# Eight of 128 first keys of an expert lookup: from gathered rows to dense products

## The chip, the cores and the metric

The kernel runs on one core of a Trainium2 chip. Times are device microseconds (us) of one execution. The core's engines are TensorE (PE, with its weight loads shown as PEld), VectorE (DVE), ScalarE (ACT), GpSimd (Pool) and SyncE (SP); 16 DMA engines move data between the chip's memory and the core.

## What is computed

The kernel computes two transformer layers and then a third block, for 256 tokens of width 1024. All but the last part of the last block is untouched here. That last part is a layer of product keys: each token has 8 heads, each head picks 16 of 16,384 experts, an expert's number being 128 times its first key plus its second key. For each of the 128 picks of a token, the kernel takes the dot product of the token with the expert's row of `expert_u`, applies Gelu, multiplies by the gate, and adds the expert's row of `expert_v` with that weight.

```
    e1 = jnp.take_along_axis(i1, ic // PEER_TOPK, axis=-1)
    e2 = jnp.take_along_axis(i2, ic % PEER_TOPK, axis=-1)
    idx = (e1 * N_KEYS + e2).reshape(T, PEER_HEADS * PEER_TOPK)
    gate = jax.nn.softmax(vc, axis=-1).reshape(T, PEER_HEADS * PEER_TOPK)

    def block(args):
        xb, ib, gb = args
        u = expert_u[ib]
        pre = jnp.einsum('td,tkd->tk', xb, u).astype(jnp.float32)
        a = jax.nn.gelu(pre, approximate=False) * gb
        return jnp.einsum('tk,tkd->td', a, expert_v[ib])
```

Each of `expert_u` and `expert_v` is 128 x 128 x 1024 numbers of 4 bytes, 64 MB.

## The kernel before

**First product.** `expert_u` is read whole. For each first key e, `u_step(e)` (L1764 and on) multiplies the 128 rows of that key with all 256 tokens on PE, in two float parts of each row (`whi` from ACT at L70, `wlo` from DVE at L73), and writes the result into the tile `GS`: GS[second key, first key, token]. PE sets the pace there.

**Second product.** `expert_v` is not read whole. There are 64 steps s of four tokens each (token s and the ones 32, 64 and 96 further on for s below 32, the second 128 tokens after that). A step has these parts:

- `gather(s)` (L1804): Pool issues four indirect DMAs, one for each token, each fetching 128 rows of 4 KB, one for each partition. They land in slots; 14 slots are taken in turn (the buffers `raw`, `whi` and `wlo` of the first product, shown as vt, and a tile vx of four).
- `spread(s)` (L1815): four small bfloat16 products copy each token's second keys to all partitions, and DVE compares them with the partition number (L86), which gives a one-hot tile of 128 x 512 under the tag `o2`.
- `extract(s)` (L1826): four products in float32 pick the picked second keys out of `GS`; then DVE picks the first key by four multiplications with a sum (L90), multiplies (L73), ACT applies Gelu (L67), DVE multiplies by the gate and makes the weight tile `w32` (L73).
- `apply(s)` (L1843): eight float32 products of 128 x 32 weights with 128 x 512 gathered values, in PSUM accumulators `acc[j][half]`, for token half j.

`store(j)` (L1848 to L1852) loads the residual `xr` on SP's queue, adds the accumulator on DVE and stores the sum. `store(0)` stands at step 31 and `store(1)` after the last step. `xr` takes buffers of the tag `o2`, of which there are three.

The order of PE, DVE, ACT and Pool is that in which the code is written: each of these engines works through its list in order. In a step the code says spread(s+2), extract(s+1), apply(s), gather(s+3). A Pool gather waits for its slot, and gather i also for the landing of gather i - 8.

## Time and profile before

| | us |
|---|---|
| median of three timed runs | 1536.12 (1535.79 to 1536.47) |
| the profiled execution: its time | 1537.89 |
| its span, first to last instruction | 1536.2 |
| first gather starts | 1182.02 |
| last gather starts | 1520.04 |

Share of the span in which each engine is busy: PE 96%, PE's weight loads 73%, DVE 69%, ACT 43%, Pool 26%. The first product takes the time up to about 1196 us, the second product the remaining 340 us, with its first gathers issued a little ahead. The shares are means over stages with different limits, so a stage is read by stretches, by timelines and by what each engine waits for. Busy time of PE is modelled: pipelined products that wait inside a run count as busy.

### The profile page before, as it was taken

What the parts mean: (1) busy time and instruction counts of PE and PEld (TensorE: products, weight loads), DVE (VectorE), ACT (ScalarE), POOL (GpSimd) and SP (SyncE); (2) the same over time, 40 slices, a digit from 0 to 9 for tenths busy, and PEclk for the clock granted to TensorE, in tenths of its full rate; (3) what the DMA queues carried; (4) which work ended last, traced back from release to release, by engine and by line L of the source; (5) the groups of instructions that cost most, each with busy time, mean ns of one, the idle gap of its engine ahead of it and who ended that gap; (6) DMA issues with size and microseconds to landing.
All of it is one profiled execution on the core that took longest, in us unless ns stands there. A gap on an engine that the chain in (4) does not pass through costs nothing.

```text
span 1536.2 us, 23739 instructions
## 1 busy us (share of the span) xinstructions
PE 1474.2 (96%) x8634; PEld 1126.9 (73%) x8634; DVE 1059.9 (69%) x2519; ACT 668.0 (43%) x1248; POOL 391.7 (26%) x516
## 2 busy tenths in 40 slices
PE   6689999999999999999999999999999999999998
PEld 5568788878988888887888888888888544444443
DVE  7887877675566676776569888999555555555554
ACT  5356555565775555647755445444444000000000
POOL 1820100010100000031110002404000777677764
PEclk9889999999999999999999999999999999999999
DMA  8514655554345555453354555555555999999998
GB/s 319 153 37 164 218 190 191 184 176 138 111 137 185 187 191 189 165 187 123 115 187 161 191 184 179 192 181 191 190 182 184 354 409 408 403 408 409 408 391 333
DMA packets 97389, 341.98 MB, mean 223 GB/s; under 512 B 12016, under 2 KB 15220, under 8 KB 96376
## 3 DMA queue, kind: packets, MB, share of 16 engines
q1 hardware_dynamic: 60120, 206.18, 39.2%
q0 software_dynamic: 36864, 134.23, 22.2%
q8 instruction: 68, 1.11, 0.3%
q14 instruction: 49, 0.40, 0.1%
q10 hardware_dynamic: 288, 0.05, 0.0%
HBM read 337.80 MB, written 2.62 MB: 222 GB/s over the span
## 4 chain that ended last, share of the span: by engine, by line
PE 69%; DMA 16%; DVE 6%; issue 4%; POOL 3%; ACT 2%; SPq 0%; POOLq 0%; DVEq 0%; ACTq 0%
PE mm L375 27%; PE mm L376 14%; DMA vt<-in_ev_dram,pidx 12%; PE acc L385 4%; PE acc L386 4%; PE acc L384 4%; PE mm L367 3%; DMA vx<-in_ev_dram,pidx 3%; PE acc L1843 2%; PE acc L247 1%; DVE wlo L73 1%; POOL vt L1804 1%; PE mm L384 1%; PE mm L385 1%; PE mm L386 1%
## 5 line engine op out<-in xcount | busy, mean ns | idle before, releaser
L375 PE MATMUL mm<-x,whi 128*128 128x512 f32 x1808 | 641.8, 399 | 0.0
L73 DVE TENSOR_TENSOR wlo<-raw,whi 128x1024 fp32r<-128x1024 f32 x345 | 434.2, 1260 | 207.6 <-ACT whi L70 194.9
L376 PE MATMUL mm<-x,wlo 128*128 128x256 f32 x1808 | 507.4, 281 | 2.0 <-DVE wlo L73 2.0
L70 ACT ACTIVATE whi<-raw 128x1024 fp32r<-128x1024 f32 x347 | 366.2, 1057 | 186.6 <-issue 92.0
L375 PEld LDWEIGHTS mm<-x,whi 128*128 128x128 f32 x1808 | 340.4, 188 | 82.5
L376 PEld LDWEIGHTS mm<-x,wlo 128*128 128x128 f32 x1808 | 341.8, 189 | 4.5 <-DVE wlo L73 2.8
L1804 POOL DMA_INDIRECT vt<-in_ev_dram,pidx x184 | 172.5, 938 | 187.1 <-DVE wlo L73 117.0
L1843 PE MATMUL acc<-vt,w 128*32 128x512 f32 x736 | 157.9, 603 | 9.0 <-DMA vt<-in_ev_dram,pidx 4.7
L67 ACT ACTIVATE pk<-pk 128x4 f32<-128x4 f32 x64 | 13.2, 205 | 314.2 <-DVE pk L73 314.2
L70 ACT ACTIVATE gs<-mm 128x256 f32<-128x256 f32 x142 | 54.6, 384 | 207.5 <-PE mm L376 207.5
L90 DVE SCALAR_TENSOR_TENSOR jk<-c,pe,mm 128x128 f32<-128x128 f32 x256 | 89.0, 348 | 72.3 <-PE mm L1826 65.4
L1826 PE MATMUL mm<-gs,o 128*128 128x128 f32 x512 | 124.6, 398 | 1.2 <-DVE o L86 1.2
L73 POOL TENSOR_TENSOR nv<-nss 128x2 f32<-128x2 f32 x5 | 1.0, 195 | 434.3 <-ACT nsq L67 434.3
L1826 PEld LDWEIGHTS mm<-gs,o 128*128 128x128 f32 x512 | 98.2, 202 | 6.2 <-issue 2.2
L1843 PEld LDWEIGHTS acc<-vt,w 128*32 128x32 f32 x736 | 27.7, 108 | 97.4 <-DMA vt<-in_ev_dram,pidx 52.6
L86 DVE TENSOR_SCALAR o<-mm,pcol 128x512 f32<-128x512 f32 x64 | 47.9, 750 | 52.0 <-PE mm L1815 52.0
L1843 PE MATMUL acc<-vx,w 128*32 128x512 f32 x288 | 71.6, 603 | 2.9 <-DMA vx<-in_ev_dram,pidx 1.3
L1804 POOL DMA_INDIRECT vx<-in_ev_dram,pidx x72 | 67.6, 938 | 23.4 <-issue 15.5
L385 PE MATMUL acc<-whi,fhl 128*128 128x512 f32 x176 | 69.9, 397 | 1.4 <-DVE fhl L73 1.4
L384 PE MATMUL acc<-whi,fhh 128*128 128x512 f32 x176 | 69.7, 400 | 1.1 <-ACT fhh L70 1.1
L386 PE MATMUL acc<-wlo,fhh 128*128 128x512 f32 x176 | 69.7, 396 | 0.0
L73 DVE TENSOR_TENSOR gs<-gs,mm 128x256 f32<-128x256 f32 x142 | 58.7, 413 | 10.8 <-ACT gs L70 10.7
(520 smaller groups left out, 2014.4 us busy)
## 6 DMA issues: line engine op xcount, KB each, us to landing
raw<-in_w_dram SPq DMA_DIRECT2D x232, 512.0 KB, 4.3
raw<-in_eu_dram SPq DMA_DIRECT2D x128, 512.0 KB, 3.2
vt<-in_ev_dram,pidx POOLq DMA_INDIRECT x184, 9.5
bcd<-in_cst_dram SPq DMA_DIRECT2D x2, 1024.0 KB, 12.5
u<-in_cst_dram SPq DMA_DIRECT2D x1, 2048.0 KB
clr<-in_cst_dram SPq DMA_DIRECT2D x2, 1024.0 KB, 6.2
vx<-in_ev_dram,pidx POOLq DMA_INDIRECT x72, 9.5
x<-in_x_dram SPq DMA_DIRECT2D x2, 512.0 KB, 4.7
```

Of the source, the lines that this page charges most:

```text
L70: return A.activation(o, i, AF.Copy)
L73: return (e or V).tensor_tensor(o, a, b, op=op)
L86: return (e or V).tensor_scalar(o, a, s1, None, op0=op0)
L90: return V.scalar_tensor_tensor(o, a, s, b, op0=op0, op1=op1, **k)
L375: T.matmul(p, hi[:, ks], x2[:, k].rearrange("p a t -> p (a t)"), start=k == 0, stop=False, skip_group_check=True)
L376: T.matmul(p[:, 0:256], lo[:, ks], xh[:, k], start=False, stop=k == 7, skip_group_check=True)
L384: T.matmul(p, xhi, hi, start=first, stop=False)
L385: T.matmul(p, xlo, hi, start=False, stop=False)
L386: T.matmul(p, xhi, lo, start=False, stop=last)
L1804: G.indirect_dma_start(v, None, evr, bass.IndirectOffsetOnAxis(ap=pidx[:, tok(s, g):tok(s, g) + 1], axis=0))
L1826: T.matmul(p[:, g * 128:(g + 1) * 128], o[:, g * 128:(g + 1) * 128], GS[:, :, tok(s, g)], start=g == 0, stop=True, skip_group_check=True)
L1843: T.matmul(acc[j][hf][32 * g:32 * g + 32], w32[:, g], vs[g][:, hf * 512:(hf + 1) * 512], start=i == 0, stop=i == 31, skip_group_check=True)
```

## The change

The rows of `expert_v` with first key 120 to 127 are no longer gathered. The gather gets a bound on its index (15,359) and skips rows above it. Instead the eight blocks of 128 rows are read whole and multiplied densely. What follows from that:

- **Layout and weights.** `GS` becomes [second key, block of 16 first keys, token, first key in the block], so that the last eight keys of eight tokens lie together. `top_e1` also makes `pe2n`, the negated second keys, and `gp`, the gate in three bfloat16 parts.
- **gate_in and gate_out**, in steps 0 to 31, eight tokens each. ACT forms the one-hot of the second keys (eight Abs of 128x128, one Relu of 128x1024), DVE the product of the first-key one-hot with the three gate parts, ACT also applies Gelu to the scaled entries of `GS`. PE multiplies the two (eight products of 24 columns), DVE adds the three parts and multiplies them into `GS`.
- **dense_in and dense**, at steps 31, 32, 36 and so on to 60. Blocks are loaded by SP, split by ACT and DVE into a high and a low part, as are their weights, and multiplied on PE (twelve products of 512 columns per block).
- **Slots.** Ten slots instead of 14, because the other four hold the one-hot and the dense block. Ten gathers are issued first, then four after each apply.
- **Order.** A step is now apply(s), gather(4), spread(s+3), extract(s+2), and then gate_in(s+1) and gate_out(s), or a dense block. The accumulators are zeroed by four products first. spread(0) and spread(1) stand in the first product at e = 124.
- **Stores.** The tag `o2` has two buffers instead of three, and `store(0)` stands at step 60, behind the last dense block.

The core of the diff:

```
+    GS = p2.tile([128, 8, 256, 16], F32, name="gs")
...
+        cp(GS[:, e // 16, :, e % 16], p[:, 256:512])
...
+    ND = 8
...
+        fixed.extend([ring_[0], ring_[1], f(ring_[4]), f(ring_[5]), f(ring_[7]), f(ring_[8])] + [vx[:, i] for i in range(4)])
+        o = ring_[2].bitcast(BF16).rearrange("p (a t k) -> p a t k", a=2, t=8)
+        return o, ring_[3], ring_[6], ring_[9]
...
+                G.indirect_dma_start(v, None, evr, bass.IndirectOffsetOnAxis(ap=pidx[:, t:t + 1], axis=0), bounds_check=128 * (128 - ND) - 1, oob_is_err=False)
...
-        o = p2.tile([128, 512], F32, name="o2", tag="o2", bufs=3)
+        o = p2.tile([128, 512], F32, name="o2", tag="o2", bufs=2)
...
+    def gate_in(n, o):
+
+        t8 = slice(8 * n, 8 * n + 8)
+        for i in range(8):
+            act(o[:, i], iota, AF.Abs, bias=pe2n[:, 8 * n + i:8 * n + i + 1])
+        act(o, o, AF.Relu, bias=1.0, scale=-1.0)
+        a = p2.tile([128, 8, 4, ND], BF16, name="ga", tag="cand", bufs=2)
+        tt(a[:, :, 3], iota[:, None, 128 - ND:128].to_broadcast([128, 8, ND]), pe1[:, t8, None].to_broadcast([128, 8, ND]), OP.is_equal)
+        mul(a[:, :, 0:3], a[:, :, 3:4].to_broadcast([128, 8, 3, ND]), gp[:, t8, :, None].to_broadcast([128, 8, 3, ND]))
+        b3 = lambda t: t[:, t8, None].to_broadcast([128, 8, ND])
+        d = GS[:, 7, t8, 16 - ND:16]
+        mul(d, d, b3(rb_p))
+        act(d, d, AF.Gelu)
+        gt_[n] = a
+
+    def gate_out(n, o):
+        a = gt_.pop(n)
+        p = bank()
+        for i in range(8):
+            T.matmul(p[:, i * 3 * ND:(i + 1) * 3 * ND], o[:, i], a[:, i, 0:3].rearrange("p k e -> p (k e)"), start=True, stop=True,
+                     skip_group_check=True)
+        V.tensor_reduce(jk[:, 0:8 * ND], p[:, 0:24 * ND].rearrange("p (t k e) -> p t e k", t=8, k=3), axis=AX.X, op=OP.add)
+        d = GS[:, 7, 8 * n:8 * n + 8, 16 - ND:16]
+        mul(d, d, jk[:, 0:8 * ND].rearrange("p (t e) -> p t e", t=8))
+
+    def dense_in(i, raw, hi, lo):
+
+        cp(hi, raw)
+        sub(lo, raw, hi.bitcast(F32))
+        if i + 1 < ND:
+            S.dma_start(raw, ev[128 - ND + i + 1])
+        ah, al = (p2.tile([128, 256], F32R, name=n_, tag=n_, bufs=1) for n_ in ("ah", "al"))
+        split(ah, al, GS[:, 7, :, 16 - ND + i])
+        gt_["d", i] = ah, al
+
+    def dense(i, hi, lo):
+        ah, al = gt_.pop(("d", i))
+        for j in range(2):
+            sl = slice(j * 128, (j + 1) * 128)
+            for hf in range(2):
+                c = slice(hf * 512, (hf + 1) * 512)
+                for l, r in ((ah, hi), (al, hi), (ah, lo)):
+                    T.matmul(acc[j][hf], l[:, sl], r[:, c], start=False, stop=False, skip_group_check=True)
...
+        gather(10)
+        S.dma_start(raw_, ev[128 - ND])
+        extract(0)
+        spread(2)
+        extract(1)
+        gate_in(0, o_[:, 0])
         for s in range(NS):
-            if s + 2 < NS:
-                spread(s + 2)
-            if s + 1 < NS:
-                ws_.append(extract(s + 1))
-            apply(s, vs.pop(0), ws_.pop(0))
-            if s + 3 < NS:
-                vs.append(gather(s + 3))
-            if s == 31:
-                store(0)
+            apply(s)
+            gather(4)
+            if s + 3 < NS:
+                spread(s + 3)
+            if s + 2 < NS:
+                extract(s + 2)
+            if s < 32:
+                if s < 31:
+                    gate_in(s + 1, o_[:, (s + 1) % 2])
+                gate_out(s, o_[:, s % 2])
+                if s == 31:
+                    dense_in(0, raw_, hi_, lo_)
+            elif s % 4 == 0:
+                i = s // 4 - 8
+                dense(i, hi_, lo_)
+                if i + 1 < ND:
+                    dense_in(i + 1, raw_, hi_, lo_)
+                else:
+                    store(0)
         store(1)
```

**What stands in a row on ACT.** The difference of its list at the start of the second product (pk is the four picked products of a step, vraw the one-hot of the second keys, c_75 the row of numbers 0 to 127, gs the eight tokens' entries of `GS`):

```order
 L70 ACTIVATE gs<-mm 128x256 x3
 L67 ACT_TABLE_LOAD
-L67 ACTIVATE pk<-pk 128x4 x64
-L2069 UNCONDITIONAL_BRANCH
+L67 ACTIVATE pk<-pk 128x4 x2
+L67 ACTIVATE vraw<-c_75,pe2n 128x128 x8
+L67 ACTIVATE vraw<-vraw 128x1024
+L67 ACTIVATE gs<-gs 128x8x8
+L67 ACTIVATE pk<-pk 128x4
```

Before there were only the 64 Gelus of pk; between two of them there are now, in the first half, eight Abs, a Relu and a Gelu on `GS`.

**What stands in a row on DVE.** Before, one step of the second product (o is the one-hot of o2, jk a scratch tile, w the weights w32, mm a PSUM bank):

```order
L86 TENSOR_SCALAR o_12508<-mm,pcol 128x512
L90 SCALAR_TENSOR_TENSOR jk,pk<-c_75,pe_8104,mm 128x128 x4
L73 TENSOR_TENSOR pk<-pk,rb_p 128x4
L73 TENSOR_TENSOR pk<-pk,pg 128x4
L73 TENSOR_TENSOR w_12523<-pk,eye 128x128
L86 TENSOR_SCALAR o_12544<-mm,pcol 128x512
```

Now one step of the first half:

```order
L86 TENSOR_SCALAR o_13147<-mm,pcol 128x512
L90 SCALAR_TENSOR_TENSOR jk,pk<-c_75,pe_8104,mm 128x120 x4
L73 TENSOR_TENSOR pk<-pk,rb_p 128x4
L73 TENSOR_TENSOR pk<-pk,pg 128x4
L73 TENSOR_TENSOR w_13162<-pk,eye 128x128
L73 TENSOR_TENSOR ga<-c_75,pe_8104 128x8x8
L73 TENSOR_TENSOR ga<-ga,gp 128x8x24
L73 TENSOR_TENSOR gs<-gs,rb_p 128x8x8
L1898 TENSOR_REDUCE jk<-mm 128x64
L73 TENSOR_TENSOR gs<-gs,jk 128x8x8
L86 TENSOR_SCALAR o_13214<-mm,pcol 128x512
```

Five operations of the gate came in behind w (ga is the first-key one-hot with the gate parts, gp the gate parts), the reduction and the last multiplication of which need PE's products of the step before.

**The end on DVE.** Before, the last two steps and the second store:

```order
L73 TENSOR_TENSOR w_14483<-pk,eye 128x128
L86 TENSOR_SCALAR o_14506<-mm,pcol 128x512
L90 SCALAR_TENSOR_TENSOR jk,pk<-c_75,pe_8104,mm 128x128 x4
L73 TENSOR_TENSOR pk<-pk,rb_p 128x4
L73 TENSOR_TENSOR pk<-pk,pg 128x4
L73 TENSOR_TENSOR w_14521<-pk,eye 128x128
L90 SCALAR_TENSOR_TENSOR jk,pk<-c_75,pe_8104,mm 128x128 x4
L73 TENSOR_TENSOR pk<-pk,rb_p 128x4
L73 TENSOR_TENSOR pk<-pk,pg 128x4
L73 TENSOR_TENSOR w_14544<-pk,eye 128x128
L73 TENSOR_TENSOR xr<-xr,acc 128x512 x2
```

Now, the last two steps and both stores:

```order
L86 TENSOR_SCALAR o_15788<-mm,pcol 128x512
L90 SCALAR_TENSOR_TENSOR jk,pk<-c_75,pe_8104,mm 128x120 x4
L73 TENSOR_TENSOR pk<-pk,rb_p 128x4
L73 TENSOR_TENSOR pk<-pk,pg 128x4
L73 TENSOR_TENSOR w_15803<-pk,eye 128x128
L73 TENSOR_TENSOR xr<-xr,acc 128x512 x2
L90 SCALAR_TENSOR_TENSOR jk,pk<-c_75,pe_8104,mm 128x120 x4
L73 TENSOR_TENSOR pk<-pk,rb_p 128x4
L73 TENSOR_TENSOR pk<-pk,pg 128x4
L73 TENSOR_TENSOR w_15852<-pk,eye 128x128
L73 TENSOR_TENSOR xr<-xr,acc 128x512 x2
```

The two additions of `store(0)` came in ahead of the last step's four reductions, its w and so its apply.

**The end on SP.** The end of its list, where each store before was two loads and then two stores:

```order
-L1850 DMA xr<-xd 128x512 x2
-L1852 DMA out_dram<-xr 128x512 x2
-L2069 UNCONDITIONAL_BRANCH
+L1988 DMA vraw<-in_ev_dram 128x1024
+L1907 DMA vraw<-in_ev_dram 128x1024 x7
+L1870 DMA xr<-xd 128x512
+L1872 DMA out_dram<-xr 128x512
+L1870 DMA xr<-xd 128x512 x2
+L1872 DMA out_dram<-xr 128x512
+L1870 DMA xr<-xd 128x512
+L1872 DMA out_dram<-xr 128x512 x2
```

The loads of the eight blocks came in, and of each store's two loads the second one now stands behind the first one's store.

## Rows read from the trace of the kernel before

**Rows 1.** The page: the span.

```profile
span 1536.2 us, 23739 instructions
```

**Rows 2.** Busy time by stretch: stretch, us, busy us of each engine (instructions), clock, DMA share, GB/s.

```profile
1370.00:1460.00 90.00, 86.01 (x478) 38.33 (x476) 47.55 (x204) 3.49 (x17) 63.85 (x69) 1.00 1.03 409
```

**Rows 3.** Pool's timeline: start us, us, engine, line, operation, tiles [idle before <-what ended it].

```profile
1198.70 0.94 POOL L1804 DMA_INDIRECT vt<-in_ev_dram,pidx  x1 [0.30 <-issue]
1199.94 0.94 POOL L1804 DMA_INDIRECT vt<-in_ev_dram,pidx  x1 [0.30 <-PE mm L1815]
...
1402.35 0.93 POOL L1804 DMA_INDIRECT vx<-in_ev_dram,pidx  x1 [0.34 <-issue]
1403.63 0.93 POOL L1804 DMA_INDIRECT vx<-in_ev_dram,pidx  x1 [0.36 <-issue]
```

**Rows 4.** Timeline of all engines, one step of the second product.

```profile
1403.13 0.35 DVE L90 SCALAR_TENSOR_TENSOR jk<-c,pe,mm 128x128 f32<-128x128 f32 x1 [1.03 <-PE mm L1826]
...
1404.19 0.16 PEld L1843 LDWEIGHTS acc<-vt,w 128*32 128x32 f32 x8 [1.02 <-DMA vt<-in_ev_dram,pidx]
...
1405.13 0.17 DVE L73 TENSOR_TENSOR pk<-pk,pg 128x4 f32<-128x4 f32 x1 [0.27 <-ACT pk L67]
1405.34 0.29 DVE L73 TENSOR_TENSOR w<-pk,eye 128x128 f32<-128x128 f32 x1
...
1406.03 0.40 PE L1815 MATMUL mm<-e2b,idb 128*128 128x128 bf16 x4
...
1411.15 0.40 PE L1815 MATMUL mm<-e2b,idb 128*128 128x128 bf16 x4
```

**Rows 5.** PE's timeline at the start of the second product.

```profile
1203.60 0.61 PE L1843 MATMUL acc<-vt,w 128*32 128x512 f32 x4
1204.14 0.40 PE L1815 MATMUL mm<-e2b,idb 128*128 128x128 bf16 x4
1204.38 1.94 PE L1826 MATMUL mm<-gs,o 128*128 128x128 f32 x8
1206.25 1.92 PE L1843 MATMUL acc<-vt,w 128*32 128x512 f32 x16
1208.11 0.40 PE L1815 MATMUL mm<-e2b,idb 128*128 128x128 bf16 x4
```

**Rows 6.** Groups of the whole run: form xcount | busy us, mean ns | idle before.

```profile
L70 ACT ACTIVATE whi<-raw 128x1024 fp32r<-128x1024 f32 x347 | 366.2, 1057 | 186.6 <-issue 92.0 <-PE mm L375 56.3 <-PE acc L385 15.9
...
L67 ACT ACTIVATE asc<-asc,nm 128x128 f32<-128x128 f32 x8 | 3.1, 386 | 0.0
...
L67 ACT ACTIVATE hsq<-ht 128x128 f32<-128x128 f32 x8 | 2.4, 307 | 0.0
...
L375 PE MATMUL mm<-x,whi 128*128 128x512 f32 x1808 | 641.8, 399 | 0.0
```

**Rows 7.** Timeline at the first store.

```profile
1360.90 0.29 DVE L73 TENSOR_TENSOR w<-pk,eye 128x128 f32<-128x128 f32 x1
...
1361.53 0.69 DVE L73 TENSOR_TENSOR xr<-xr,acc 128x512 f32<-128x512 f32 x1 [0.33 <-PE acc L1843]
...
1364.87 0.69 DVE L73 TENSOR_TENSOR xr<-xr,acc 128x512 f32<-128x512 f32 x1 [2.66 <-DMA xr<-xd]
...
1368.33 0.29 DVE L73 TENSOR_TENSOR w<-pk,eye 128x128 f32<-128x128 f32 x1
```

**Rows 8.** DMA from 1180 us on: queue, kind: packets, MB, share; issues, KB, us to landing.

```profile
q0 software_dynamic: 36864, 134.23, 95.5%
...
xr<-xd SPq DMA_DIRECT2D x4, 256.0 KB, 6.2
out_dram<-xr SPq DMA_DIRECT2D x4, 256.0 KB, 4.1
```

**Rows 9.** Timeline at the end.

```profile
1525.09 1.90 PE L1843 MATMUL acc<-vx,w 128*32 128x512 f32 x10 [0.23 <-DMA vx<-in_ev_dram,pidx]
...
1530.16 1.90 PE L1843 MATMUL acc<-vt,w 128*32 128x512 f32 x10 [0.22 <-DMA vt<-in_ev_dram,pidx]
```

More of the change, by code (lines that the diff above doesn't have):

```diff
@@ L1639, in tile_kernel @@
     pcol = p2.tile([128, 1], F32, name="pcol")
+    pe2n = p2.tile([128, 256], F32, name="pe2n")
+    gp = p2.tile([128, 256, 3], BF16, name="gp")
     eye = p2.tile([128, 32, 32], BF16, name="eye")
@@ L1670, in q_step @@
             mm_x2(p, hi, lo)
-        qT = GS[:, 90 + m % 5]
+        qT = flat(5)[:, m % 5 * 256:(m % 5 + 1) * 256]
         if m < 2:
@@ L1785, in tile_kernel, with fix, gather @@
     toks = lambda t, s: t[:, 128 * (s // 32) + s % 32:128 * (s // 32) + s % 32 + 97:32]
[L1786 to L1806 removed]
+    fixed = []
+    def fix():
+        ring_ = [ring.tile([128, 1024], dt, name="v" + k, tag=k, bufs=n) for k, n, dt in (("raw", 4, F32), ("whi", 3, F32R), ("wlo", 3, F32R))
+                 for _ in range(n)]
+        vx = acts.tile([128, 4, 1024], F32, name="vx", tag="x2")
+        f = lambda t: t.bitcast(F32)
+        fixed.extend([ring_[0], ring_[1], f(ring_[4]), f(ring_[5]), f(ring_[7]), f(ring_[8])] + [vx[:, i] for i in range(4)])
+        o = ring_[2].bitcast(BF16).rearrange("p (a t k) -> p a t k", a=2, t=8)
+        return o, ring_[3], ring_[6], ring_[9]
+    def slot():
+        return fixed[len(vs) % len(fixed)]
+    vs = []
+    def gather(n):
+        for _ in range(n):
+            i = len(vs)
+            if i < 4 * NS:
+                v = slot()
+                t = tok(i // 4, i % 4)
+                G.indirect_dma_start(v, None, evr, bass.IndirectOffsetOnAxis(ap=pidx[:, t:t + 1], axis=0), bounds_check=128 * (128 - ND) - 1, oob_is_err=False)
+                vs.append(v)
     xs_ = {}
@@ L1836, in extract, with apply @@
         mul(w32, pk[:, :, None].to_broadcast([128, 4, 32]), eye[:, s % 32, None, :].to_broadcast([128, 4, 32]))
-        return w32
-    def apply(s, vs, w32):
+        ws_.append(w32)
+    ws_ = []
+    def apply(s):
         j, i = s // 32, s % 32
+        w32 = ws_.pop(0)
         for hf in range(2):
             for g in range(4):
-                T.matmul(acc[j][hf][32 * g:32 * g + 32], w32[:, g], vs[g][:, hf * 512:(hf + 1) * 512],
-                         start=i == 0, stop=i == 31, skip_group_check=True)
+                T.matmul(acc[j][hf][32 * g:32 * g + 32], w32[:, g], vs[4 * s + g][:, hf * 512:(hf + 1) * 512],
+                         start=False, stop=False, skip_group_check=True)
     def store(j):
@@ L1848, in store @@
             c = slice(hf * 512, (hf + 1) * 512)
-            xr = p2.tile([128, 512], F32, name="xr", tag="o2", bufs=3)
+            xr = p2.tile([128, 512], F32, name="xr", tag="o2", bufs=2)
             S.dma_start(xr, xd[j * 128:(j + 1) * 128, c])
@@ L1910, in tile_kernel @@
                 run_bg(0.85)
+            if e == 124:
+                spread(0)
+                spread(1)
         u_join()
         acc = out_accum()
-        vs = [gather(s) for s in range(3)]
-        spread(0)
-        spread(1)
-        ws_ = [extract(0)]
+        o_, raw_, hi_, lo_ = fix()
+        for j in range(2):
+            for hf in range(2):
+                T.matmul(acc[j][hf], eye[:, 0, 1:2].to_broadcast([128, 128]), eye.rearrange("p a b -> p (a b)")[:, 0:512], start=True, stop=False, skip_group_check=True)
+        gather(10)
[4 more added lines that the diff above has]
+        gate_in(0, o_[:, 0])
         for s in range(NS):
+            apply(s)
+            gather(4)
+            if s + 3 < NS:
+                spread(s + 3)
             if s + 2 < NS:
-                spread(s + 2)
-            if s + 1 < NS:
-                ws_.append(extract(s + 1))
-            apply(s, vs.pop(0), ws_.pop(0))
-            if s + 3 < NS:
-                vs.append(gather(s + 3))
-            if s == 31:
-                store(0)
+                extract(s + 2)
[12 more added lines that the diff above has]
+                    store(0)
         store(1)
```

38 lines of the change are left out of this document (13 added, 25 removed).

## The prediction

> **What bounds the kernel now.** I read the page first: 1536.2 us on one core [rows 1]. The profiled run took 1537.9 us and the median of the three timed runs is 1536.1, so a change of the span is added to 1536.1. About 0.2% (3 us) is what a measurement of this kernel can tell from no change. The change touches the last 340 us, so I then read busy time by stretch of that stage: from 1370 to 1460 DMA is full (share 1.03 at 409 GB/s), PE is nearly always "busy" (86 of 90 us), DVE about half, Pool 0.71, and ACT 0.04 [rows 2]. Third, Pool's timeline: the gathers start 1.24 us apart where nothing holds them (1198.70, 1199.94) and 1.28 us apart later (1402.35, 1403.63) [rows 3]. 512 KB in 1.28 us is 409 GB/s: DMA sets the pace, and Pool stands only 3% below it. Fourth, all engines in one step: four gathers make 5.12 us (spread at 1406.03, the next at 1411.15), and in every step PE waits 1.02 us inside apply for a gathered tile [rows 4]; its busy share hides that. Without that wait PE needs 3.97 us a step: spread 0.24, extract 1.87, apply 1.86 [rows 5]. So PE has 1.15 us to spare per step, DVE more than 2, ACT nearly all. The second product runs from apply(0), done at 1204.2 [rows 5], to the last apply, 1530.16 + 1.90 [rows 9].
>
> **What is saved: the gathers.** First keys 120 to 127 leave the gather. From the reference's inputs I count 2,355 of 32,768 rows, 7.2% (8 of 128 keys would be 6.25%). If every dropped row saves its share, DMA needs 1.28 x 0.928 = 1.19 us per gather, and Pool, at 1.24, becomes the bound: at most 256 x 0.04 = 10 us can be won. Against that stand eight dense blocks of 512 KB, 1.28 us each at the rate of [rows 2], together 10.2 us of the same DMA. On traffic alone the change is about even. For a gather with clipped indices the trace has no row; I take Pool's 1.24 us and keep 1.19 and 1.28 for DMA as bounds.
>
> **First half, steady step.** Each step s below 32 now also rescales the dense weights of 8 tokens: on ACT eight 128x128 Abs, one 128x1024 Relu and a small Gelu, on PE eight narrow matmuls, on DVE five small operations. Summed by engine this fits: ACT about 4.0 of 5.12 us, DVE 2.7 + 1.4, PE 3.97 + 0.5. But the engines work in order, and there is a ring: ACT's Abs stand behind the Gelu of extract(s+2), PE's gate_out(s+1) waits for the Relu behind them, and apply(s+2), spread and extract(s+4) stand behind gate_out(s+1) on PE. One turn spans two steps:
> - extract done to Gelu done: from the first reduction at 1403.13 to 1405.13, where DVE goes on behind the Gelu, 2.0 us [rows 4];
> - eight Abs: a 128x128 group of ACT took 2.4 us for eight without an operand per partition, 3.1 with one [rows 6]. I take 2.5, nearer to the first, because these groups have no chain between their members. Relu: 1.06, as whi of the same shape [rows 6];
> - eight matmuls of 24 columns: four of spread take 0.24 [rows 5], so 0.5;
> - apply 1.86, spread 0.24, extract 1.87 [rows 5]; handovers between engines 0.2 in all, an estimate: the 0.27 that DVE waits there holds a whole Gelu and two of them [rows 4].
>
> The sum is 10.2 us for two steps, 5.1 a step. In the trace the 31 steps from apply(0) to apply(31), whose end lets the first store's add start at 1361.53 [rows 7], took 157.3 us, 5.07 a step. So the shorter gathers bring **nothing** here: +1 us, with -2 (2.4 for the Abs) to +10 (3.1) as ends.
>
> **First half, conflicts.** The weights that are rescaled lie in GS, and extract reads whole GS columns of four tokens (s + 32g, g = 0 to 3) while the gate rescales tokens 8n to 8n+7. Where extract(s+2) needs a token of group n = s, its matmul g waits for that group's Gelu on ACT, which stands behind Abs and Relu. Solving 8s <= s+2+32g <= 8s+7 gives s = 0 (g = 0), 4 (g = 1), 9 (g = 2), 13 and 14 (g = 3). There the ring closes in one step, not two: 2.0 + 2.5 + 1.06 + 0.25 (a Gelu is under the 0.27 of [rows 4]) + 0.1 = 5.9 us, plus what is left of extract (0.47 per g): 7.8, 7.3, 6.85, 6.4 and 6.4, against 5.1: +2.7, +2.2, +1.75, +1.3, +1.3 = **+9.2**. Where the token falls in group n = s - 1 (s = 1, 5, 6, 10, 15) it waits for the last multiply of gate_out on DVE, behind w32 (2.5 us after extract's end [rows 4]) and five small operations of 0.17 to 0.35, the smallest and largest of [rows 4]: about 3.9 us against 2.6 of PE work before it (0.5 + 1.86 + 0.24); less 0.47 per g this is 1.3, 0.85 twice, 0.4 and 0, of which I take 3. The start adds 2: four zeroing matmuls, and extract(1) and gate_in(0) before apply(0). Together **+14**; 9 if the second kind hides. This cannot be won back later: before, 14 slots of gathered tiles ran ahead; now there are 10, and Pool at 1.24 stands only 0.14 us a step below the ring.
>
> **Second half.** Per four steps PE has 4 x 3.97 = 15.9 us plus one dense block of twelve 512-column matmuls: 2.8 us if they scale as two thirds of the 0.355 us in which the u stage does 512 + 256 columns, 4.3 at the whole of it [rows 6]. That is 18.7 to 20.2, under DMA: 16 gathers and a load, 20.3 (1.19), 21.1 (1.24) or 21.8 (1.28), where it was 20.5. Splitting a block into high and low parts costs ACT 1.06 us [rows 6] and something more, DVE about the same; both lie in idle time, once in four steps. 31 steps at 21.1/4 are 163.5 us, against 165.6 in the trace from apply(31) at 1361.4 to apply(62) at 1527.0 [rows 7, 9], in which the first store cost about 2 (w32 at 1360.90 and 1368.33, 7.4 us apart, DVE having waited 2.66 us for an xr load [rows 7]). That store is gone from the middle, other interruptions stay: **-1**, ends -5 and +5.
>
> On the DMA side, q0 moved 36,864 packets for 256 gathers, 144 = 16 x 9 each [rows 8]: sixteen engines with equal shares. What a dropped row is worth depends on which engine it leaves idle. The Trainium skill, page "DMA: Bandwidth & Descriptors", section "The descriptor swizzle", says that of a 128-partition transfer each engine writes 8 fixed partitions; heads lie on blocks of 16 partitions here, so by that rule some engines lose almost no rows (the fullest keeps 7.8 of 8 on average), a gather costs 1.25 instead of 1.24, and the half +1 more. No row of before decides it.
>
> **The end.** store(0) moves from step 31 to step 60, behind the last dense block, and o2 has two buffers, not three; one holds step 63's one-hot, so SP runs load xr, store, load xr, store in a row. DVE has both adds ahead of extract(63)'s reductions, so w32(63) and apply(63) stand behind them. The chain from extract(62)'s end: load 6.2, add 0.69, store 4.1, load 6.2 or, since the gathers end meanwhile, less (2 as a low estimate: its bytes alone are 0.6 us at 409 GB/s), add 0.69 [rows 7, 8], then 2.5 to w32 [rows 4] and 1.9 of apply: 18.1 to 22.3 us. Undisturbed, apply(63) would end three steps of 5.3 less 2.1 (spread and extract) later: 13.8. So it is late by 4.3 to 8.5; I take **+6**. After it store(1) has one more load in the chain: **+1** (0 to 3).
>
> **Hidden.** The stores of the u stage into GS in strides, its spare reductions and the gate's bfloat16 parts lie on ACT and DVE beside 8 x 0.355 = 2.8 us of PE work per step [rows 6]; I cost them at nothing, and if strided writes doubled the 0.4 us of one step they would still fit under it.
>
> **Sum.** +1 + 14 - 1 + 6 + 1 = +21 us: 1536.1 + 21 = **1557**.
>
> **Rivals.**
> - *The gate hides and the gathers shrink (faster).* The mechanism is the ring: if Abs are issued at 0.28 us or less and the conflicts fall into PE's spare 1.15 us, the first half goes by Pool's floor, 4.96 a step, 31 x 0.11 = -3.4; the second half at 1.19 gives -5; the store chain +3 at its cheapest. 1531. For it: ACT has 96% of the stage idle. Against it: order, not load, makes the ring. 0.07; 0.04 more for ending within 3 us of before.
> - *Dropped rows save nothing.* Sixteen equal shares of packets [rows 8] end together only if all lose alike; if in each gather some engine keeps its full share, DMA stays at 1.28 and four steps with a load take 21.8: +5 in the second half, 1562. For it: by my count the dropped rows lie unevenly, and among blocks of eight rows some block keeps all eight in nearly every gather. Against it: eight gathers in flight let one engine's shortfall meet another's. 0.17. The Trainium skill's rule on the swizzle, above, stands for this rival in the weaker form, 1558.
> - *A clipped gather costs Pool more.* Pool has 0.30 us between two gathers [rows 3]; the new bound and a register move each lie there. At +0.15, 1.39 a gather, 5.56 a step, the steps without a conflict lose 0.4: about +15 more, 1572. It decides from 1.28 up. 0.12.
> - *The chains are as I say:* 0.60.
>
> The likeliest is 1557. Ends of the ring (-3, +9), the second half (-4, +6) and the store (-3, +4) do not fall together; the range is 1542 to 1575. Faster by over 0.2%: 0.07; within: 0.04; slower: 0.89.
>
> **What would show it.** In the changed profile: Abs in runs of eight, about 2.5 us, with PE's gate_out waiting on ACT's Relu in most first-half steps; extract waiting on ACT's GS Gelu near steps 0, 4, 9, 13 and 14, with steps of 6.4 to 7.8 us; gathers 1.24 apart in bursts with gaps after them; DVE waiting several us for xr in front of the last reductions. I am wrong if Pool's gathers run evenly in the first half, if the step there is below 5, or if the last apply follows the one before by 5 us.

## The result, and the profile after

The changed kernel took 1557.59 us (median, 1556.24 to 1558.99) against 1535.95 (1534.87 to 1536.47): a ratio of 1.014, 95% interval 1.0127 to 1.0152, slower by 21.6 us. (The two profiled executions differ by 19.7 us in span, because that of the kernel before, at 1537.89, was above its median; the stretches below add up to 19.7.) The forecast was 1557. The sum came out; its terms for the first half, the second half and the end did not, and they nearly cancelled. The rest of this document is about those terms.

The page of the changed kernel (parts 1, 3 and 5; the answer to [rows 1, 6]):

```profile
span 1555.9 us, 25284 instructions
PE 1453.6 (93%) x8989; PEld 1118.1 (72%) x8990; DVE 1132.0 (73%) x2707; ACT 814.7 (52%) x1584; POOL 412.9 (27%) x516
DMA packets 98550, 336.64 MB, mean 216 GB/s; under 512 B 14499, under 2 KB 17703, under 8 KB 97528
q0 software_dynamic: 36864, 124.60, 21.4%
...
L70 ACT ACTIVATE gs<-mm 128x256 f32<-128x256 f32 x142 | 87.0, 613 | 186.7 <-PE mm L376 186.7
L1822 POOL DMA_INDIRECT vx<-in_ev_dram,pidx x100 | 99.9, 999 | 33.9 <-issue 21.4
L1843 PE MATMUL mm<-gs,o 128*128 128x128 f32 x512 | 73.6, 285 | 10.6 <-ACT gs L67 7.5
L67 ACT ACTIVATE vraw<-c,pe2n 128x128 bf16<-128x128 f32 x256 | 77.8, 386 | 0.0
```

What to see: the gather queue q0 still has 36,864 packets, as in [rows 8], but 9.6 MB less; a skipped row is still a packet, a small one (4 bytes; q0 has 2,355 more of these than before, which is the count of skipped rows). One gather takes Pool 0.999 us on average in this group; in [rows 3] it was 0.94. Extract (L1843 now) takes PE 73.6 us in all. The Abs of the gate are 77.8/32 = 2.43 us for eight, as the prediction took them.

Pool's timeline in the first half (the answer to [rows 3]) and the stretch with the dense blocks (the answer to [rows 2]):

```profile
1303.33 0.99 POOL L1822 DMA_INDIRECT vwhi<-in_ev_dram,pidx  x1 [0.30 <-issue]
1304.63 0.99 POOL L1822 DMA_INDIRECT vwhi<-in_ev_dram,pidx  x1 [0.31 <-PE mm L1896]
...
1380.00:1535.00 155.00, 145.00 (x891) 64.72 (x883) 88.31 (x350) 16.97 (x42) 115.03 (x116) 1.00 1.00 381
```

Here the gathers start 1.294 us apart with nothing but the usual 0.30 between them: Pool issues without a pause. In the stretch with the dense blocks DMA moves 381 GB/s where it moved 409 [rows 2]; its busy share of 1.00 does not tell the two bounds apart, since it is 1.00 as well in the run below with a bound and no dense blocks, in which Pool never waits for anything from w32(0) on. Where no slot is awaited the bound is Pool now, at a pace that is 1% slower than DMA's 1.28 was. Where a slot is awaited, Pool stops, and its stops come on top.

The marks that divide the second product are the writes of the weights w32. Of the kernel before, three that were not among the rows (the fourth is in [rows 7]), then of the changed kernel:

```profile
1201.94 0.29 DVE L73 TENSOR_TENSOR w<-pk,eye 128x128 f32<-128x128 f32 x1
...
1519.75 0.29 DVE L73 TENSOR_TENSOR w<-pk,eye 128x128 f32<-128x128 f32 x1
...
1525.39 0.29 DVE L73 TENSOR_TENSOR w<-pk,eye 128x128 f32<-128x128 f32 x1
```

```profile
1200.95 0.29 DVE L73 TENSOR_TENSOR w<-pk,eye 128x128 f32<-128x128 f32 x1
...
1367.38 0.29 DVE L73 TENSOR_TENSOR w<-pk,eye 128x128 f32<-128x128 f32 x1
...
1530.48 0.29 DVE L73 TENSOR_TENSOR w<-pk,eye 128x128 f32<-128x128 f32 x1
...
1547.79 0.29 DVE L73 TENSOR_TENSOR w<-pk,eye 128x128 f32<-128x128 f32 x1
```

| stretch, us | before | after | difference | forecast |
|---|---|---|---|---|
| up to w32(0) | 1201.9 | 1201.0 | -1.0 | |
| w32(0) to w32(32) | 159.0 | 166.4 | +7.5 | +15 |
| w32(32) to w32(62) | 158.9 | 163.1 | +4.3 | -1 |
| w32(62) to w32(63) | 5.6 | 17.3 | +11.7 | +7 with the next |
| w32(63) to the end of the span | 10.8 | 8.1 | -2.7 | |
| sum | | | +19.7 | +21 |

The end of the changed kernel, timeline of all engines:

```profile
1528.25 0.33 SPq L1870 DMA_DIRECT2D xr<-xd  x1
...
1535.79 0.69 DVE L73 TENSOR_TENSOR xr<-xr,acc 128x512 f32<-128x512 f32 x1 [5.02 <-DMA xr<-xd]
...
1536.50 0.34 SPq L1872 DMA_DIRECT2D out_dram<-xr  x1
...
1542.22 0.79 SPq L1870 DMA_DIRECT2D xr<-xd  x2
1545.03 0.69 DVE L73 TENSOR_TENSOR xr<-xr,acc 128x512 f32<-128x512 f32 x1 [8.55 <-DMA xr<-xd]
...
1548.14 1.07 PE L1863 MATMUL acc<-vwhi,w 128*32 128x512 f32 x2 [8.56 <-DVE w L73]
...
1551.85 0.69 DVE L73 TENSOR_TENSOR xr<-xr,acc 128x512 f32<-128x512 f32 x1 [0.94 <-PE acc L1863]
```

This is the chain of the prediction, step for step: load (7.5 us to the add), add, store (5.7 us until the next load may start), load (2.8), add, and only then the last step's reductions on DVE; PE waited 8.56 us for w. The last gather had started at 1534.98.

The forecast's +6 is for the end of the last apply and its +1 for what follows. The last add, which waits for that apply, divides the two; of the kernel before:

```profile
1532.10 0.69 DVE L73 TENSOR_TENSOR xr<-xr,acc 128x512 f32<-128x512 f32 x1 [0.17 <-PE acc L1843]
```

From w32(62) to the last add it is 12.4 us before and 21.4 after, +9.0; from there to the end of the span it is 4.1 both times. The last apply itself became slower too. Busy time by stretch around it, in the changed kernel:

```profile
1548.00:1552.00 4.00, 3.64 (x16) 0.59 (x16) 0.92 (x3) 0.00 (x0) 0.00 (x0) 0.50 0.24 86
```

After PE's 8.56 us without work the granted clock is 0.50 (1.2 of 2.4 GHz), and the apply takes 3.64 us; before, an apply took 1.9 [rows 5]. The chain on DVE therefore cost 1.7 us more than the wait.

### The profile page after: what moved, and what is told of

Same layout as the page of the kernel before. It is cut to its first block, busy times and chain, and to the rows that moved or that the text cites. A ratio compares the mean times of both kernels' runs of the same rounds, so it can differ in the third digit from the quotient of the medians.

```text
span 1555.9 us, 25284 instructions
## 1 busy us (share of the span) xinstructions
PE 1453.6 (93%) x8989; PEld 1118.1 (72%) x8990; DVE 1132.0 (73%) x2707; ACT 814.7 (52%) x1584; POOL 412.9 (27%) x516
## 2 busy tenths in 40 slices
DMA packets 98550, 336.64 MB, mean 216 GB/s; under 512 B 14499, under 2 KB 17703, under 8 KB 97528
## 3 DMA queue, kind: packets, MB, share of 16 engines
q0 software_dynamic: 36864, 124.60, 21.4%
## 4 chain that ended last, share of the span: by engine, by line
PE 67%; DMA 11%; DVE 10%; ACT 5%; issue 4%; POOL 2%; SPq 0%; POOLq 0%; DVEq 0%; ACTq 0%
PE mm L375 25%; PE mm L376 13%; PE acc L386 4%; PE acc L385 4%; PE acc L384 4%; PE acc L1863 3%; PE mm L367 3%; DMA vx<-in_ev_dram,pidx 3%; DVE wlo L73 2%; DMA vwhi<-in_ev_dram,pidx 2%; DMA vraw<-in_ev_dram,pidx 2%; ACT vraw L67 2%; DMA vwlo<-in_ev_dram,pidx 2%; PE mm L1843 2%; PE acc L247 1%
## 5 line engine op out<-in xcount | busy, mean ns | idle before, releaser
L70 ACT ACTIVATE gs<-mm 128x256 f32<-128x256 f32 x142 | 87.0, 613 | 186.7 <-PE mm L376 186.7
L1822 POOL DMA_INDIRECT vx<-in_ev_dram,pidx x100 | 99.9, 999 | 33.9 <-issue 21.4
L1863 PE MATMUL acc<-vx,w 128*32 128x512 f32 x400 | 102.6, 621 | 5.7 <-DMA vx<-in_ev_dram,pidx 5.5
L90 DVE SCALAR_TENSOR_TENSOR jk<-c,pe,mm 128x120 f32<-128x120 f32 x256 | 86.8, 339 | 26.0 <-PE mm L1896 10.0
L73 DVE TENSOR_TENSOR gs<-gs,mm 128x256 f32<-128x256 f32 x142 | 85.7, 603 | 10.9 <-ACT gs L70 10.8
L1822 POOL DMA_INDIRECT vraw<-in_ev_dram,pidx x52 | 52.9, 1018 | 128.2 <-DVE wlo L73 110.7
L1843 PE MATMUL mm<-gs,o 128*128 128x128 f32 x512 | 73.6, 285 | 10.6 <-ACT gs L67 7.5
L67 ACT ACTIVATE vraw<-c,pe2n 128x128 bf16<-128x128 f32 x256 | 77.8, 386 | 0.0
L1863 PE MATMUL acc<-vwhi,w 128*32 128x512 f32 x208 | 63.5, 635 | 12.1 <-DVE w L73 8.6
L1843 PEld LDWEIGHTS mm<-gs,o 128*128 128x128 f32 x512 | 63.3, 193 | 13.3 <-ACT gs L67 8.2
```

The lines of the kernel that those rows point to most:

```text
L67: return A.activation(o, i, f, **k)
L70: return A.activation(o, i, AF.Copy)
L73: return (e or V).tensor_tensor(o, a, b, op=op)
L90: return V.scalar_tensor_tensor(o, a, s, b, op0=op0, op1=op1, **k)
L1822: G.indirect_dma_start(v, None, evr, bass.IndirectOffsetOnAxis(ap=pidx[:, t:t + 1], axis=0), bounds_check=128 * (128 - ND) - 1, oob_is_err ...
L1843: T.matmul(p[:, g * 128:(g + 1) * 128], o[:, g * 128:(g + 1) * 128], GS[:, :, tok(s, g)], start=g == 0, stop=True, skip_group_check=True)
```

## The experiments

In all, twelve kernels. Times are medians of four to ten executions, beside runs of the kernel before on the same chip. Where an experiment is set against the changed kernel, that is 1557.59; it was not run beside the experiments, but the kernel before was, and apart from one chip, named below, its medians there (1536.26 and 1536.18) lie within 0.4 us of the 1535.95 above. Each trace is of one execution.

**store(0) behind the last reductions.**

```
-                else:
-                    store(0)
+            if s == 62:
+                store(0)
```

> One edit to the changed kernel: store(0) stands at step 62, behind the last step's reductions, instead of step 60 ahead of them. In the changed kernel DVE waited 8.55 us for the second xr load while the last four reductions stood behind it, and w32(63) came 17.3 us after w32(62). Theory (the order on DVE holds the last apply): w32(63) comes about 5 us after w32(62), the last apply follows the last gather's landing, near 1543; but four loads and stores in a row with two buffers are left at the end, so only 3 to 6 us of the 8 are won: about 1553. Rival (the last gathers hold the end anyway, the last gather starting at 1535): under 2 us.

Measured: 1553.89 (1551.99 to 1557.16), ratio to before 1.012 (1.01 to 1.0139): 3.7 less. Its timeline at the end:

```profile
1529.64 0.29 DVE L73 TENSOR_TENSOR w<-pk,eye 128x128 f32<-128x128 f32 x1
...
1535.33 0.29 DVE L73 TENSOR_TENSOR w<-pk,eye 128x128 f32<-128x128 f32 x1
...
1542.61 0.62 PE L1863 MATMUL acc<-vwlo,w 128*32 128x512 f32 x1 [0.52 <-DMA vwlo<-in_ev_dram,pidx]
...
1546.16 0.69 DVE L73 TENSOR_TENSOR xr<-xr,acc 128x512 f32<-128x512 f32 x1 [0.85 <-DMA xr<-xd]
```

w32(63) now comes 5.7 us after w32(62), as before the change, and the last apply waits for a gathered tile. So the order on DVE did hold the last apply. That only 4 of the 11.7 us are won is mostly not for the stores: the last gathered rows now set the end. By the last packets of the gather queue in the traces, the last row lands 6.5 us before the end of the span in the kernel before, 13.6 in the changed kernel and 8.1 here. So 5.5 of 7.1 us are repaired in this execution (the fastest of its four), and at most 1.6 are left for the loads and stores through two buffers, of which the last add waits 0.85.

**A gate order without conflicts.**

```
+    GO = [*range(16, 32), 3, 7, 11, 15, 0, 4, 8, 12, 2, 6, 10, 14, 1, 5, 9, 13]
...
     def gate_in(n, o):
...
+        n = GO[n]
...
     def gate_out(n, o):
+        n = GO[n]
```

> One edit to the changed kernel: the gate takes the groups of eight tokens in an order in which no extract needs a token of a group in work (groups 16 to 31 first, then 3, 7, 11, 15, 0, 4, 8, 12, 2, 6, 10, 14, 1, 5, 9, 13). Theory (conflicts cost time): PE's waits of extract on ACT and DVE for GS (7.5 and 2.6 us in the changed kernel) go, gathers lose their gaps of the first half, 5 to 8 us less: about 1551. Rival A (the ring of Gelu, Abs, Relu and gate_out sets the pace in any case): nothing, 1557. Rival B (Pool's 1.294 us a gather sets it and the conflicts were in its shadow): 0 to 3 us less.

Measured: 1556.15 (1550.65 to 1557.81), ratio to before 1.0115 (1.009 to 1.014): 1.4 less, within the scatter. PE's waits from 1204 to 1367 (engine, line, waited for: us, times, longest), in the changed kernel and then in this one:

```profile
PE mm L1896 <- ACT vraw L67: 17.1, 21, 2.1
PE mm L1843 <- ACT gs L67: 7.5, 4, 3.8
PE mm L1843 <- DVE gs L73: 2.6, 4, 0.7
```

```profile
PE mm L1899 <- ACT vraw L67: 12.6, 19, 2.2
PE mm L1899 <- DVE pk L73: 2.7, 1, 2.7
```

The conflicts were there, at four places of each kind, 10.1 us of PE's waiting, and all of them are gone here. Yet w32(0) to w32(32) falls only from 166.4 to 164.0. (Two other runs keep the changed kernel's first half: 167.6 with store(0) late, 168.2 with the dense blocks in parts. The run with all three edits has the new order: 165.0. So the order wins 1 to 4 us of the stretch.) That is rival B: the waits lay mostly in the shadow of Pool's pace. Between w32(0) and w32(32) Pool stood still, beyond its usual 0.30, for only 6.9 us in the changed kernel, 4.4 of them at the start, and for 3.4 here, all at the start. Pool's timeline of the changed kernel there, the second stop of this run, and the kernel before with the changed kernel's bound (below):

```profile
1201.43 0.99 POOL L1822 DMA_INDIRECT vx<-in_ev_dram,pidx  x1 [0.30 <-issue]
1203.47 0.99 POOL L1822 DMA_INDIRECT vraw<-in_ev_dram,pidx  x1 [1.05 <-PE acc L1863]
...
1207.39 0.99 POOL L1822 DMA_INDIRECT vwhi<-in_ev_dram,pidx  x1 [0.30 <-issue]
1212.36 0.99 POOL L1822 DMA_INDIRECT vwlo<-in_ev_dram,pidx  x1 [3.98 <-PE acc L1863]
```

```profile
1213.46 0.98 POOL L1822 DMA_INDIRECT vwlo<-in_ev_dram,pidx  x1 [2.90 <-PE acc L1863]
```

```profile
1206.50 0.99 POOL L1804 DMA_INDIRECT vt<-in_ev_dram,pidx  x1 [0.30 <-issue]
1207.80 0.99 POOL L1804 DMA_INDIRECT vt<-in_ev_dram,pidx  x1 [0.30 <-issue]
1209.09 0.99 POOL L1804 DMA_INDIRECT vt<-in_ev_dram,pidx  x1 [0.30 <-PE mm L1826]
```

With ten slots Pool stands still until the first and again until the second apply is done, 0.75 + 3.68 = 4.4 us beyond its 0.30; with 14 it never stops there. The second stop is 1.1 us shorter without conflicts, so the conflict of step 0 is part of it. The stops of Pool, 6.9 us, nearly make up the 7.5 us by which the stretch grew: what Pool loses was not won back in it. How much of the start is the ten slots and how much the new order of the start was not told apart (the run meant for that says nothing, below).

**Dense blocks in four parts.**

```
-            elif s % 4 == 0:
+            elif s < 60:
                 i = s // 4 - 8
-                dense(i, hi_, lo_)
+                dense(i, hi_, lo_, (s % 4,))     # 3 of the 12 products
+                if s % 4 == 3:
                     dense_in(i + 1, raw_, hi_, lo_)
```

> One edit to the changed kernel: the twelve products of a dense block are done three in each of four steps instead of twelve in one; the last block stays whole in step 60, with store(0) behind it. Theory (the block of 2.9 us on PE keeps slots from coming free, and Pool's gathers have a gap of 0.6 to 1.4 us at each block, six of them): 4 to 6 us less, about 1552. Rival (those gaps come from DMA, by the dense block's load): same time as the changed kernel.

Measured: 1554.74 (1553.15 to 1557.41), ratio to before 1.0115 (1.0097 to 1.0132): 2.9 less, though the spread of the runs overlaps that of the changed kernel. w32(32) to w32(62) takes 159.7 here and 161.2 with all three edits; with whole blocks it takes 163.1 (changed kernel), 161.7 (store(0) late) and 163.2 (gate order). So the split wins about 2 us of the stretch, and PE's block of 12 products is a part of the second half's loss; that it is most of it is not shown. The changed kernel's Pool behind the block of step 36, and beside DVE's split of a later block:

```profile
1404.71 0.98 POOL L1822 DMA_INDIRECT vx<-in_ev_dram,pidx  x1 [1.68 <-PE acc L1863]
...
1423.88 1.23 DVE L73 TENSOR_TENSOR vwlo<-vraw,vwhi 128x1024 fp32r<-128x1024 f32 x1 [1.23 <-ACT vwhi L70]
1424.11 1.86 POOL L1822 DMA_INDIRECT vwhi<-in_ev_dram,pidx  x1 [0.30 <-issue]
```

The first gather waits for its slot: such stops are 3.6 us of the stretch in the changed kernel and 2.8 here. The second shows another loss, which neither the expectation nor its rival has. A gather that Pool starts while DVE's split of 1.23 us runs, 0.1 to 1.1 us into it, ends only 0.85 to 0.87 us after the split does; this holds for every such gather in the traces of the kernels with dense blocks and a bound, and it then takes up to 1.99 instead of 0.99 us. Prolonged gathers are 2.5 us of the stretch in the changed kernel (five gathers, three of them beside a split) and 3.5 here (seven, beside seven of the eight splits), which takes back part of what the edit wins.

**The three edits together**, the last block split too and store(0) at step 62.

> The three edits together on the changed kernel: gate in the conflict-free order, dense blocks split over their four steps (the last one too), store(0) at step 62. Theory (the three losses are separate, and under them Pool's 1.294 us a gather sets the pace): 4.5 + 6 + 5 less, about 1542, still 5 above the kernel before. If the gathers' pace were set by the gate, it would stay above 1548.

Measured: 1545.98 (1542.46 to 1552.48), ratio to before 1.0054 (1.0034 to 1.0073): 11.6 less than the changed kernel, where the single edits add up to 8.0. So no edit takes away what another wins, and about half of the 21.6 us is repaired; 1542 was too low by 4. The surplus of 3.6 lies within the scatter of the four medians (this run's executions are 10 us apart), and this run also splits the last block, which the single edit did not.

**And the residuals loaded early**, into tiles that are free by then:

```
+                if s == 44:
+                    S.dma_start(res_, xd[0:128, :])
+                if s == 60:
+                    S.dma_start(raw_, xd[128:256, :])
...
-            xr = p2.tile([128, 512], F32, name="xr", tag="o2", bufs=2)
-            S.dma_start(xr, xd[j * 128:(j + 1) * 128, c])
```

> The three edits together and, beyond them, both residuals loaded early into tiles that are free by then (step 44 into the one-hot's, step 60 into the dense block's), so that a store is two additions and two stores without a load. Theory (after the last apply about 5 us went to xr loads and stores in a chain): 4 to 6 us less than the three edits alone, about 1541. Rival (the last gathers' landings set the end): no less than 1545.

Inconclusive as a time. This run and the last three runs of this section fell on a chip on which the kernel before itself took 1582.69 us at a granted clock of 0.95 (0.99 elsewhere); why is not known. There it took 1597.30, a ratio of 1.0107 (1.0075 to 1.014). In the profiles, the stretch from the start of the last gather to the end of the span is 12.4 us (1582.57 to 1595.0), against 16.1 with the three edits alone (1534.58 to 1550.7): 3.7 less, near the 4 to 6 expected. But most of that is not the residuals. The last gather's rows land 5.5 us after its start here and 8.0 there, by the last packets of the gather queue (the gathers start 1.55 us apart on this chip, 1.33 to 1.36 there; with fewer of them under way the last may land sooner, which is not shown); from that landing to the end of the span it is 7.0 against 8.1. What loading early wins is thus 1.1 us in these two profiles, and what it would make of the time on another chip is open.

**No bound on the index.**

```
-... axis=0), bounds_check=128 * (128 - ND) - 1, oob_is_err=False)
+... axis=0))
```

> The changed kernel without the bound on the gather's index: all 128 rows of each gather move again (rows of the last eight first keys are fetched and get weight zero); all else stays. Theory (the bound costs Pool 0.05 us a gather): Pool's gather takes 0.94 instead of 0.99 us, spacing where nothing holds it 1.24 instead of 1.294, and DMA becomes the bound again at 1.28, with 10 us of dense loads on top in the second half: between the same and 5 us more, 1557 to 1563. Rival (skipped rows cost Pool the time): also 0.94, told apart by the kernel before with a bound that skips nothing.

Measured: 1562.01 (1558.09 to 1564.38), ratio to before 1.0167 (1.0143 to 1.0191). 4.4 more than with the skip, within what was expected. The group of Pool on its page:

```profile
L1822 POOL DMA_INDIRECT vx<-in_ev_dram,pidx x100 | 94.8, 948 | 40.2 <-issue 17.7
```

A gather takes 0.948 us again, but all rows and the eight blocks pass through DMA.

**The kernel before with a bound**, once one that skips nothing (16,383) and once the changed kernel's (15,359).

```
+... axis=0), bounds_check=128 * 128 - 1, oob_is_err=False)
```

> The kernel before with a bound on the gather's index that no index exceeds (16,383), nothing skipped. Theory (the bound itself costs Pool 0.05 us): gather 0.99 us, 1.294 apart, Pool instead of DMA sets the pace at +0.014 us a gather: 3 to 4 us more, 1539.5. Rival (only skipped rows cost it): gather 0.94, 1.28 apart, 1536.

> The kernel before with the changed kernel's bound (15,359), and no dense products: the last eight first keys' part of the output is left out. Theory (Pool's 1.294 us a gather is the pace, whatever DMA saves): as with the bound that skips nothing, 1539.5, PE's wait for gathered tiles unchanged. Rival (the dropped 7.2% of the rows shorten the gathers to 1.19 to 1.25): 1525 to 1530.

Measured: 1536.95 (1535.47 to 1540.12), ratio 1.0012 (1.0003 to 1.0022), and 1532.24 (1530.02 to 1534.54), ratio 0.9969 (0.9957 to 0.9982). Pool's groups, of the one that skips nothing and then of the one that skips:

```profile
L1804 POOL DMA_INDIRECT vt<-in_ev_dram,pidx x184 | 182.7, 993 | 176.2 <-DVE wlo L73 116.9
```

```profile
L1804 POOL DMA_INDIRECT vt<-in_ev_dram,pidx x184 | 182.5, 992 | 173.6 <-DVE wlo L73 116.9
```

The bound itself, not the skipped rows, costs Pool 0.05 us a gather. In time it cost 0.8 us by the medians (0.5 to 3.4 by the interval), less than the 3 to 4 expected: with all its interruptions the kernel before had its gathers 1.290 us apart from w32(0) to w32(32) and 1.312 from there to w32(62), not 1.28, and with the bound they are 1.297 and 1.318 apart. Skipping won 3.9 us against the kernel before (2.8 to 6.6 by the interval), less than the rival's 6 to 11 and more than my nothing. It lies between w32(32) and w32(62), 158.8 us with the bound alone and 154.7 with skipping: the gathers are then 1.294 apart, and the interruptions of the kernel before are gone. This run sets the ceiling of the idea for a gather with a bound: with eight of 128 first keys gone from the gathers and nothing put in their place (their part of the output is left out), 3.9 us are won. The dense products would have to cost less than that.

**The layout of GS alone, in the kernel before.**

```
-    GS = p2.tile([128, 128, 256], F32, name="gs")
+    GS = p2.tile([128, 8, 256, 16], F32, name="gs")
```

> The kernel before with the changed kernel's layout of GS alone. In the changed kernel extract took 1.11 us of PE instead of 1.9, and each copy into GS 0.61 instead of 0.38 us on ACT and 0.60 instead of 0.41 on DVE. Theory (the layout makes extract short, DMA sets the pace of the second product, PE that of the first): extract 1.1 us, PE's wait inside apply 1.02 up to about 1.8 us, time the same within 2 us, 1536. Rival (the slower copies show in the first product, 128 x 0.2): some us more; or the shorter step helps the end: some us less.

Measured: 1536.70 (1535.40 to 1539.41), ratio 1.0004 (0.9992 to 1.0016): no change. PE's groups in the second product, of the kernel before and then of this one:

```profile
L1843 PE MATMUL acc<-vt,w 128*32 128x512 f32 x736 | 157.9, 603 | 9.0 <-DMA vt<-in_ev_dram,pidx 4.7
...
L1826 PE MATMUL mm<-gs,o 128*128 128x128 f32 x512 | 124.6, 398 | 1.2 <-DVE o L86 1.2
```

```profile
L1844 PE MATMUL acc<-vt,w 128*32 128x512 f32 x736 | 181.4, 603 | 15.9 <-DMA vt<-in_ev_dram,pidx 14.5 <-DVE w L73 1.4
...
L1827 PE MATMUL mm<-gs,o 128*128 128x128 f32 x512 | 71.1, 282 | 1.6 <-DVE o L86 1.6
```

Extract falls to 71.1/64 = 1.11 us a step from 1.87 [rows 5], and PE waits the more for DMA, as the theory said: before the runs of products (9.0 to 15.9 us in this group) and inside them, where waiting counts as busy (157.9 to 181.4). The slower copies into GS (0.61 us against 0.38 on ACT) are hidden in the first product, where PE sets the pace: the time stays the same.

**What a skipped row saves where DMA is the bound.** Two kernels, with 12 slots and 62 unused loads of 512 KB besides, one without skipping and one with it:

```
+            if 2 <= s:
+                V.tensor_copy(jk[:, 0:1], quarter[0][:, 2 + s % 2, 0:1])
+            if s < NS - 2:
+                S.dma_start(quarter[0][:, 2 + s % 2], ev[s])
```

> A measurement of DMA alone, in pair with the next. The kernel before with a bound that skips nothing (16,383), 12 slots, and in 62 steps a load of one 512 KB block by SP that is not used (DVE reads one column of it), so that DMA, not Pool, is the bound: per step four gathers and a load, 5 x 1.28 = 6.4 us; about 1536 + 79 = 1615.

> As the run before, but with the changed kernel's bound (15,359): 2,355 of 32,768 rows are skipped, and the last eight first keys' part of the output is left out. What does a skipped row save where DMA is the bound? If all rows count alike, 7.2% of 328 us: 24 us less than the run before. If each engine writes fixed partitions, as the Trainium skill's page DMA: Bandwidth & Descriptors states under The descriptor swizzle, the fullest engine keeps 7.79 of 8 rows: 8 to 9 us less. If each gather waits for its own fullest engine: nothing.

Measured: 1616.51 (1615.55 to 1619.62) and 1604.62 (1601.55 to 1607.27), the same chip for both. (That 1616.51 is near the 1615 expected says little, since the kernel before took 1582.69 on this chip and not 1536.) Busy time from 1260 to 1560, without and with skipping:

```profile
1260.00:1560.00 300.00, 248.89 (x1289) 107.52 (x1288) 131.97 (x600) 9.50 (x46) 180.70 (x183) 0.98 1.02 407
```

```profile
1260.00:1560.00 300.00, 255.23 (x1338) 112.24 (x1334) 135.69 (x621) 9.95 (x48) 188.72 (x191) 0.99 1.02 396
```

DMA is the bound in both (share 1.02). Skipping wins 11.9 us: half of the 24 of an even saving, nearer to the 8 to 9 of fixed partitions, and with 396 instead of 407 GB/s DMA moves less per unit of time although the mean share of the engines is as full. An even saving is excluded, and so is none. The rule of the Trainium skill, page "DMA: Bandwidth & Descriptors", section "The descriptor swizzle", points the right way. That it is the cause is not shown: the trace does not name the engine of a packet, and a share that stays at 1.02 shows no engine idle; in the trace the 4 KB packets of the gathers only become a little longer, 167.6 instead of 164.9 ns on average.

**Ten slots in the kernel before.**

> The kernel before with the changed kernel's ten slots (the same ten tiles in the same order) instead of 14, all else as before. In the changed kernel the first half took 166 us from w32(0) to w32(32) against 159, and 164 with the conflict-free gate; 5 us of the difference lie in the first five steps, where Pool stood still 2.6 to 4.8 us before its fourteenth gather. Theory (ten slots let Pool stand still until the first apply is done, and with Pool or DMA as the pace that is never won back): 3 to 6 us more, with the gap before the eleventh or a later gather in the trace. Rival (the order at the start, with extract(1) and gate_in(0) ahead of apply(0), is the cause): the same time, 1536.

This one says nothing: 2037.69 us. I gave the ten tiles in turn but left three steps of gathers ahead, so that the third step's gathers write tiles that earlier steps still need: rows are overwritten before their use, and the steps come 13.3 us apart. What ten slots cost by themselves stays open; the gaps at the start, shown above, are all the evidence.

## Why the prediction was right, and where it was not

**The side and the size were right, the sum by luck in part.** Its likeliest case, that chains and not loads decide, held at the end and, weakly, in the first half; the pace of the middle was another, Pool's. The first half came out 7.5 us below its forecast, the second half 5.3 above and the end 2.0 above, which nearly cancels.

**The ring (5.1 us a step forecast).** The term that failed is extract: I took 1.87 us from [rows 5], and the new layout makes it 1.11. The narrow products took 0.36 instead of 0.5. With these the ring is 2.0 + 2.43 + 1.06 + 0.36 + 1.86 + 0.24 + 1.1 + 0.2 = 9.25 us for two steps, 4.6 a step, under Pool's 4 x 1.294 = 5.18. So the ring was real (PE waited 17.1 us for the Relu) but, by this sum, not the pace. I had named the layout among the hidden edits and never asked whether it made a read cheaper. The Trainium skill, page "SBUF — State Buffer", section "Door 1: The DMA port swizzle", notes that SBUF is read in lines of 16 bytes and that each new line costs; before, each of the 128 numbers that extract reads lay 1 KB from the last, now 16 lie together. The runs agree in direction: with the layout alone an instruction of extract takes 282 ns against 398 (PE runs each product as two); that the lines are the reason is not shown.

**Pool.** The prediction's third rival, a clipped gather that costs Pool more, came true at +0.055 us, not +0.15, and in the gather itself, not in the 0.30 between two. I put its threshold at 1.28 and its chance at 0.12; the pace of 1.294 passed that threshold, but its price of 15 us did not come. It cost little by itself (0.8 us), but it leaves Pool no room to make up for a stop.

**Conflicts and start (+14 forecast, +7.5 measured for the whole first half with the ring).** The places were right: extract waited for ACT's Gelu at four of the five places named and for DVE's multiplication at four of five. The waits were near the forecast too, 10.1 us against 12.2. Their price was not: the order without conflicts won 1.4 of the time and 2.4 of the first half, since Pool's gathers ran on into free slots meanwhile, and Pool stood still for only 2.5 us after the start. That time which PE loses could not be won back was the wrong step; it holds for Pool's time. The start, for which I took 2, cost Pool 4.4, part of it by the first conflict.

**Second half (-1 forecast, +4.3 measured).** I compared sums over four steps, 18.7 to 20.2 for PE against 21.1 for DMA. But the pace was Pool's: within four steps the twelve products stand in one block, and ten slots do not carry Pool across it, which stopped it for 3.6 us. And I put the splitting of a block at nothing, as DVE is idle enough for it; yet gathers beside DVE's split took up to 1.92 us, and prolonged gathers cost Pool 2.5 in this stretch. Splitting PE's block won about 2 us of the stretch.

**The end (+7 forecast, +9.0 measured).** The order of the chain was right; the load and the store under the gathers took 7.5 and 5.7 us instead of 6.2 and 4.1. The sum lacked the last apply's 1.7 us at a granted clock of 0.50, and its +1 for the second store did not come (4.1 us from the last add to the end, before and after).

**The gathers.** That the gain is limited by Pool was right, at 1.294 instead of 1.24; the ceiling was about 4 us, not 10.

## What to carry to other kernels

Before work is taken off a bound, run the kernel with that work simply left out: here it showed a ceiling of 3.9 us, since the next bound, Pool's 1.294, stood 1% from DMA's 1.28. When a sum per engine fits, still follow the order of each queue: a lump of a few us on one engine costs if the buffers ahead of it cover less, and an operation that waits for a transfer holds everything behind it on its engine, as the two additions here held the last apply. Look at what an engine's operation does to another engine's beside it, even where both have idle time, as DVE's split and Pool's gathers here. And price a change of layout on every reader and writer of it, not only on the one for which it is made.
